# Weights rounded by casting transfers, their low parts made by adding transfers

## The chip, the cores and the metric

One core of a Trainium2 chip runs the kernel. The engines named in the profile are PE (the tensor engine, with its weight loads as PEld), DVE (vector), ACT (scalar), POOL (GpSimd) and SP (the engine that issues the transfers; SPq is its queue). The metric is the device time of one execution in microseconds (µs), lower is better.

## The reference

A two-layer encoder on x of 512 tokens by 1024 features, in float32. Each layer normalises its input, projects it with one matrix `w_in` (1024 by 4608) and splits the columns among three groups of heads: differential attention (A), retention with decays in both directions (B) and a pooling mixer (C). Each group is gated, and `w_out` (1536 by 1024) maps the three back onto the residual stream.

```
for l in range(2):
    h = rmsnorm(x, norm_w[l])
    aq, ak, av, ag, bq, bk, bv, bg, cu, cg = split(h @ w_in[l])
    o_a = diff_attention(aq, ak, av, rel_bias, lam, subln_w) * silu(ag)
    o_b = retention(bq, bk, bv, decay) * silu(bg)
    o_c = multiscale_pool(cu, pool_w, pool_scale) * silu(cg)
    x = x + concat(o_a, o_b, o_c) @ w_out[l]
out = rmsnorm(x, final_norm_w)
```

## The kernel before

**Two parts of every operand.** Matmuls run in the reduced type float32r. To keep float32's accuracy every operand is split in two: a high part, the value rounded to float32r, and a low part, the value minus the high part. A product is three matmuls (`mm3`): high by high, high by low, low by high. Weights are held as `wh` and `wl`.

**Granules.** The weights come in 96 granules of 128 partitions by 1024 elements, 0.5 MB each, in the order in which the units of a layer need them (the table `ORDERS`; a unit's name tells the columns of `w_in` or the blocks of `w_out`). A granule of a gate, a query or a key is 128 columns by all 1024 rows (eight pieces of 512 B in a partition); one of the values `bv`, `av` (four granules a unit) or of `w_out` is 256 rows by 512 columns (two pieces of 2 KB). The first unit of the program is `bv` of layer 0, granules 1 to 4.

**How one granule is made** (`emit_granule`): SP issues a transfer into a raw tile `wraw` (2 buffers), ACT casts it to `wh`, DVE subtracts `wh` from `wraw` into `wl` (`split`). `wh` and `wl` have 5 slots each (`WBUFS`). So the raw data of the next two granules is fetched while their slots are still in use. A unit takes its granules with `take`; 24 matmuls of 512 columns read a granule.

**What sets the order.** The program is first recorded; a list scheduler (`Recorder.schedule`) then fixes the order on every engine from planned costs (`cost`) and priorities, and gives each tile its slot. At run time each engine goes through its own list in order and waits where a semaphore tells it to: an instruction that waits holds up all that stand behind it on its engine. This holds for SP's and POOL's transfers too.

**Names around the change.** `hh`, `hl` are the parts of the normalised, transposed input; layer 0 runs on x transposed (`T<-in_xT_w`) with the weight of the norm alone, and each token's factor, the reciprocal root mean square, is applied to the products afterwards. That factor is made from `x` by ACT (squares), DVE and POOL (`st`, a power of -1/2, once for each of four token tiles), kept in `edge`, written to memory as `row` and read back on all partitions as `rb`. `pj` (3 banks), `lg` (2), `tp` (2) and `ov` (1) are the accumulation banks of the tensor engine. The heads' own norms take the same way (`st4`, `row`, `hn`). `wide` holds bias or decay tables, one buffer.

Of the kernel before, what the change touches and what calls it, by code (L numbers as in the profile page):

```python
# [9 lines left out]
F32 = mybir.dt.float32  # L10
# [19 lines left out]
# Order in which the units of a layer are recorded. An output unit is named by the pairs of 128-row blocks of w_out that it takes  # L30
# (A: P Q, B: R S, C: T U) and its half of the columns.
# [4 lines left out]
ORDERS = [o.split() for o in ORDERS]  # L36
PAIRS = {"P": ("A", 0), "Q": ("A", 2), "R": ("B", 0), "S": ("B", 2), "T": ("C", 0), "U": ("C", 2)}

# how far the units of a kind are moved ahead
# [4 lines left out]
# The kernel body is recorded first, on tiles that have no place yet. A list scheduler then fixes the order in which  # L44
# every engine issues its instructions and the slot each tile takes, and the program is emitted in that order.
# [17 lines left out]
class View:  # L63
    """Part of a recorded tile: partitions p0..p1, free offsets idx, and the steps that lead to it."""
# [32 lines left out]
    def window(self, row, first, pattern):  # L97
        """DRAM only: elements of a row from first on, by an access pattern of its own."""
        return View(self.base, self.p0, self.p1, self.idx, self.steps + (("window", row, first, pattern),))

    def spread(self, n):
        """Every element n times, along a new last axis."""
        return View(self.base, self.p0, self.p1, np.repeat(self.idx[..., None], n, -1), self.steps + (("spread", n),))
# [47 lines left out]
class Recorder:  # L151
# [9 lines left out]
    def add(self, name, engine, method, args, kw):  # L161
# [4 lines left out]
        ins = [v for v in list(args[1:]) + [x for k, x in kw.items() if k != "accum_out"] if isinstance(v, View)]  # L166
# [34 lines left out]
    def schedule(self):  # L201
# [39 lines left out]
        def ready(op):  # L241
            """A PSUM bank serves one engine at a time."""
# [55 lines left out]
WARM = 16  # matmuls on zeros at the start  # L298
QUEUE = 8  # transfers under way in a queue
FINE = 2  # weight granules of the first columns that come in two parts  # L300
# [3 lines left out]
def cost(engine, method, args, kw):  # L304
    """What an instruction weighs for the list scheduler: until its result stands, and on its engine."""
# [3 lines left out]
    if engine == "PE":  # L309
# [6 lines left out]
        return t, t  # L316
    if engine == "SP":
# [33 lines left out]
def record(ins: dict, out: bass.AP):  # L351
    nc = Recorder()
    x_d = ins["x"][0]
    w_in, w_out = ins["w_in"], ins["w_out"]
# [46 lines left out]
    def g_cols(l, c):  # L401
        return [w_in[l, :, c:c + P].rearrange("(k p) c -> p k c", p=P)]

    def g_tok(l, c):
        return [w_in[l, g * 256:(g + 1) * 256, c:c + 512].rearrange("(k p) c -> p k c", p=P) for g in range(4)]

    def g_out(l, e0, half):
        return w_out[l, e0:e0 + 256, HALF[half]].rearrange("(k p) c -> p k c", p=P)

    def unit_granules(l, u):  # L410
        if u in ("bv", "av"):
            return g_tok(l, BV if u == "bv" else AV)
        kind, i = u[:-1], int(u[-1])
        if kind in ("bg", "ag", "cu", "cg"):
            return g_cols(l, {"bg": BG, "ag": AG, "cu": CU, "cg": CG}[kind] + i * P)
        if kind == "bqk":
            return g_cols(l, BQ + i * P) + g_cols(l, BK + i * P)
        if kind == "qk":
            return g_cols(l, AQ + i * P) + g_cols(l, AK + i * P)
        if kind[0] == "o":  # L420
            return [g_out(l, "PQRSTU".index(c) * 256, i) for c in kind[1:]]
        return []

    granules = [g for l in range(DEPTH) for u in ORDERS[l] for g in unit_granules(l, u)]
# [3 lines left out]
    def emit_granule(parts=1):  # L428
        src = granules[len(wt)]
        shp = [P, src.shape[1], src.shape[2]]  # L430
# [28 lines left out]
    def square(t, half, junk, part=None):  # L459
        """Mean square of token tile t: the share of one half of its columns, or of a quarter in the second half."""  # L460
# [14 lines left out]
    def scaled(t, wb, dst, half):  # L475
        """One half of the columns of the rmsnorm of token tile t."""
        c = HALF[half]
        nc.vector.scalar_tensor_tensor(dst[:, c], xt[t][half], stats[t][:, 2:3], wb[:, c], op0=ALU.mult, op1=ALU.mult)

    def transpose4(src, step=None):  # L480
        """Four 128-column blocks of src, each transposed, in one bank."""
# [22 lines left out]
    def mm_stacked(ps, qk, m, cols):  # L504
        """Full product of slot m's query columns with its keys: both query parts lie stacked on partitions."""
# [16 lines left out]
    def stack_halves(dst, slots, src, scale, dup):  # L522
        """Split the 64 rows of each half of src. Without dup the low part goes to the other partition half of
        the same slot; with dup both parts take a slot each, present on both partition halves."""
# [13 lines left out]
    def headnorm(ov, scale, g):  # L538
        """ov * scale * rsqrt(mean over partitions of ov^2 + eps) * g"""
# [17 lines left out]
    def out_half(ms, half, after=None, before_end=None):  # L557
        """before_end: the last token tile comes in two quarters of the columns, and this follows the first."""
# [555 lines left out]
```

## Time and profile before

| | before |
|---|---|
| median of 3 runs, µs | 682.0 (681.04 to 682.2) |
| span of the profiled execution, µs | 679.9 |
| PE busy, µs | 659.5 |
| DVE busy, µs | 500.7 |
| ACT busy, µs | 353.9 |
| POOL busy, µs | 30.3 |
| DMA queue of SP, share of 16 engines | 36.3% |
| DMA, mean GB/s | 106 |

The profile is of one execution, whose span from the first to the last instruction stands above; the median is of whole runs. A busy engine is one that executes: waiting does not count. Matmuls overlap in their pipeline, so one that is listed with 0.39 µs starts 0.23 µs after the one before.

### The profile page before, as it was taken

Reading aid. Unit: us, or ns where it says so; the run is one execution under the profiler, and the core shown is the slowest. Engines: PE = TensorE matmul, PEld = TensorE weight load, DVE = VectorE, ACT = ScalarE, POOL = GpSimd, SP = SyncE. Lnnn points to the kernel's source line nnn. Section 1 sums busy time; section 2 is a strip of 40 time slices with the busy share of each in tenths; the row PEclk is TensorE's granted clock in tenths of the full one; section 3 lists DMA queues with packets and bytes.
Section 4 is the critical chain, followed back from the end, with each engine's and each line's share of the span. In section 5 each row is a group of like instructions: output and inputs, shape, how many; then the busy total and the mean of one; then the engine's idle time right before and its main releaser. Section 6 shows DMA issues by size and latency. Waiting matters only on the chain.

```text
span 679.9 us, 8912 instructions
## 1 busy us (share of the span) xinstructions
PE 659.5 (97%) x3171; PEld 541.1 (80%) x3171; DVE 500.7 (74%) x954; ACT 353.9 (52%) x701; POOL 30.3 (4%) x51
## 2 busy tenths in 40 slices
PE   9969999999999999999999999899999999999996
PEld 7757887878788888887888888688888887888785
DVE  5468987787787998976574779767568957887733
ACT  7525673434376866553443756344447765655321
POOL 0000000000000000001010000000000000000011
PEclk9979999999999999999999999999999999999999
DMA  9447444323326223243322423532342143224302
GB/s 325 147 127 186 139 115 117 110 94 78 90 50 181 77 91 105 69 115 91 115 63 78 139 64 88 131 118 71 95 122 65 50 150 97 71 92 90 99 31 94
DMA packets 85141, 71.86 MB, mean 106 GB/s; under 512 B 6004, under 2 KB 67604, under 8 KB 85096
## 3 DMA queue, kind: packets, MB, share of 16 engines
q1 hardware_dynamic: 85096, 71.29, 36.3%
q8 instruction: 25, 0.41, 0.2%
q14 instruction: 20, 0.16, 0.1%
HBM read 69.09 MB, written 2.18 MB: 105 GB/s over the span
## 4 chain that ended last, share of the span: by engine, by line
PE 78%; DMA 10%; DVE 6%; issue 2%; ACT 2%; SPq 1%; POOL 0%; POOLq 0%; DVEq 0%; ACTq 0%
PE pj L1051 64%; PE lg L1051 6%; PE ov L1051 4%; PE tp L1051 4%; DMA hn<-row 3%; DMA wide<-dd 2%; DVE qk L1051 1%; DMA row<-edge 1%; DVE soft L1051 1%; DMA wraw<-in_w_in 1%; DVE wl L1051 1%; DMA cols<-in_scales 1%; DMA T<-in_xT_w 1%; DMA x<-in_x 1%; ACT soft L1051 1%
## 5 line engine op out<-in xcount | busy, mean ns | idle before, releaser
L1051 PE MATMUL pj<-hh,wh 128*128 128x512 f32 x448 | 178.5, 400 | 7.9 <-ACT wh L1051 6.5
L1051 PE MATMUL pj<-hl,wh 128*128 128x512 f32 x448 | 177.5, 397 | 0.0
L1051 PE MATMUL pj<-hh,wl 128*128 128x512 f32 x448 | 176.9, 396 | 0.0
L1051 ACT CAST wh<-wraw 128x1024 fp32r<-128x1024 f32 (+1 forms) x97 | 100.8, 1039 | 106.9 <-PE pj L1051 75.8
L1051 DVE TENSOR_TENSOR wl<-wraw,wh 128x1024 fp32r<-128x1024 f32 (+1 forms) x97 | 117.3, 1210 | 29.7 <-ACT wh L1051 29.1
L1051 PEld LDWEIGHTS pj<-hh,wh 128*128 128x128 f32 x448 | 84.7, 189 | 27.1 <-ACT wh L1051 7.0
L1051 PEld LDWEIGHTS pj<-hh,wl 128*128 128x128 f32 x448 | 84.6, 189 | 18.6
L1051 PEld LDWEIGHTS pj<-hl,wh 128*128 128x128 f32 x448 | 84.7, 189 | 17.7
L1051 PE MATMUL pj<-wh,mAC 128*128 128x512 f32 (+1 forms) x264 | 87.5, 391 | 0.0
L1051 ACT ACTIVATE soft<-soft,sm 128x512 f32<-128x512 f32 x96 | 67.8, 718 | 33.9 <-DVE sm L1051 33.5
L1051 DVE TENSOR_TENSOR x<-x,pj 128x512 f32<-128x512 f32 (+1 forms) x65 | 43.6, 675 | 23.2 <-PE pj L1051 22.8
L1051 PEld LDWEIGHTS pj<-wh,mAC 128*128 128x128 f32 x264 | 49.0, 188 | 10.3
L1051 PE MATMUL lg<-qk 128*128 128x512 f32 (+1 forms) x192 | 51.4, 361 | 1.5 <-DVE soft L1051 1.5
L1051 PE MATMUL pj<-wl,mAC 128*128 128x512 f32 (+1 forms) x132 | 51.4, 389 | 0.0
L1051 POOL TENSOR_TENSOR st<-st,neghalf 128x4 f32<-128x4 f32 (+1 forms) x28 | 25.1, 896 | 477.3 <-DVE st L1051 379.2
L1051 DVE CUSTOM_DVE_ANT_0 soft<-lg,wide 128x512 f32<-128x512 f32 x64 | 43.3, 687 | 1.9 <-PE lg L1051 0.3
L1051 PE MATMUL pj<-wh,mB 128*128 128x512 f32 (+1 forms) x136 | 44.5, 383 | 0.0
L1051 PE MATMUL pj<-wh,hl 128*128 128x512 f32 x104 | 41.4, 398 | 0.0
L1051 PE MATMUL pj<-wh,hh 128*128 128x512 f32 x104 | 41.3, 398 | 0.0
L1051 PE MATMUL pj<-wl,hh 128*128 128x512 f32 x104 | 41.2, 396 | 0.0
L1051 PEld LDWEIGHTS lg<-qk 128*128 128x128 f32 x192 | 32.5, 188 | 9.6 <-DVE soft L1051 2.5
L1051 PE MATMUL ov<-T,vh 128*128 128x256 f32 x192 | 39.1, 284 | 0.4 <-DVE og L1051 0.3
(151 smaller groups left out, 949.7 us busy)
## 6 DMA issues: line engine op xcount, KB each, us to landing
wraw<-in_w_in SPq DMA_DIRECT2D x71, 512.0 KB, 4.6
wraw<-in_w_out SPq DMA_DIRECT2D x24, 512.0 KB, 4.1
hn<-row SPq DMA_DIRECT2D x16, 256.0 KB, 3.9
wide<-gd SPq DMA_DIRECT2D x8, 448.0 KB, 4.0
T<-in_xT_w SPq DMA_DIRECT2D x8, 258.0 KB, 4.1
x<-in_x SPq DMA_DIRECT2D x8, 256.0 KB, 5.0
wide<-dd SPq DMA_DIRECT2D x8, 256.0 KB, 4.8
out<-T SPq DMA_DIRECT2D x8, 256.0 KB, 2.1
```

The costliest lines, as they stand in the source:

```text
L1051: op.inst = getattr(getattr(tc.nc, name), method)(*[real(a) for a in op.args], **{k: real(v) for k, v in op.kw.items()})
```

## The change

From the fifth granule on, no raw tile is used. POOL issues a transfer from memory straight into `wh`; source and destination differ in type, so the transfer rounds. ACT then writes minus `wh` into `wl`. POOL issues a second transfer of the same source into `wl` that adds to what is there: the value minus the high part. DVE has no part in it. The first four granules are still made as before. The host lays all granules out as one array `wg`, in the order of use, so that a partition's 1024 elements lie in one row of 4 KB. The scheduler gets a planned cost for a POOL transfer, and an adding transfer is recorded as a reader of its destination.

```diff
+def weight_granules():
+    out = []
+    for l in range(DEPTH):
+        for u in ORDERS[l]:
...
+                out += [("w_in", l, (256 * g, BV if u == "bv" else AV), (2, 512)) for g in range(4)]
...
-        ins = [v for v in list(args[1:]) + [x for k, x in kw.items() if k != "accum_out"] if isinstance(v, View)]
+        kw_ins = [args[0]] if "accum_op" in kw else []
+        ins = [v for v in list(args[1:]) + [x for k, x in kw.items() if k != "accum_out"] + kw_ins if isinstance(v, View)]
...
+    if engine == "POOL" and method == "dma_start":
+        return 5500, 1500
...
-        src = granules[len(wt)]
-        shp = [P, src.shape[1], src.shape[2]]
+        at, (nk, nc_) = granules[len(wt)]
+        shp = [P, nk, nc_]
+        src = ins["wg"][at].rearrange("p (k c) -> p k c", k=nk)
+        if len(wt) >= 4:
+            hi = sb("wh", shp, WBUFS, F32R)
+            lo = sb("wl", shp, WBUFS, F32R)
+            nc.gpsimd.dma_start(hi, src)
+            nc.scalar.activation(lo, hi.bitcast(F32), AF.Copy, scale=-1.0)
+            nc.gpsimd.dma_start(lo, src, accum_op=ALU.add)
+            wt.append((hi, lo))
+            return
...
+    wg = np.empty((len(weight_granules()), P, 1024), np.float32)
+    for g, (name, l, (r, c), (nk, n)) in zip(wg, weight_granules()):
+        g[:] = np.asarray(inputs[name])[l, r:r + nk * P, c:c + n].reshape(nk, P, n).transpose(1, 0, 2).reshape(P, 1024)
+    a["wg"] = wg
```

**SP, the first 33 µs.** Numbers behind a name tell tiles apart. `row` and `rb` are the tokens' factor on its way out and back. Before:

```order
L1051 DMA x_0_242<-in_x 128x512
L1051 DMA x_0_253<-in_x 128x512
L1051 DMA wraw_262<-in_w_in 128x8x128
L1051 DMA wraw_276<-in_w_in 128x8x128
L1051 DMA soft_287<-in_decay 8x2
L1051 DMA row_319<-edge_112 128x4x1
L1051 DMA rb_339<-row_319 128x512
L1051 DMA wraw_348<-in_w_in 128x8x128
L1051 DMA wraw_397<-in_w_in 128x8x128
L1051 DMA wraw_408<-in_w_in 128x8x128
```

Now:

```order
L1059 DMA x_0_251<-in_x 128x512
L1059 DMA x_0_264<-in_x 128x512
L1059 DMA wraw_274<-in_pool_w 128x4x128
L1059 DMA wraw_288<-in_pool_w 128x4x128
L1059 DMA soft_299<-in_decay 8x2
L1059 DMA row_353<-edge_114 128x4x1
L1059 DMA rb_377<-row_353 128x512
L1059 DMA dd_476<-T_449 8x1024
L1059 DMA wide_493<-dd_476 128x2x256
```

The loads of weights that stood ahead of and behind `row` and `rb` are gone from SP; two early loads of `pool_w` stand in the first two places.

**POOL, the same place.** `st` with `neghalf` is the power for one token tile, `u` a margin that is zeroed; both lists begin behind the constants. Before:

```order
L1051 MEMSET u_67 128x8 x2
L1051 ISA
L1051 TENSOR_TENSOR st_172<-st_172,neghalf_65 128x1
L1051 TENSOR_TENSOR st_199<-st_199,neghalf_65 128x1
L1051 TENSOR_TENSOR st_279<-st_279,neghalf_65 128x1
L1051 TENSOR_TENSOR st_295<-st_295,neghalf_65 128x1
L1051 MEMSET u_511 128x8 x2
L1051 MEMSET u_576 128x8 x2
```

Now:

```order
L1059 DMA wh_67<-in_wg 128x1024
L1059 MEMSET u_93 128x8 x2
L1059 DMA wl_137<-in_wg 128x1024
L1059 DMA wh_187<-in_wg 128x1024
L1059 ISA
L1059 TENSOR_TENSOR st_177<-st_177,neghalf_65 128x1
L1059 DMA wh_247<-in_wg 128x1024
L1059 TENSOR_TENSOR st_206<-st_206,neghalf_65 128x1
L1059 DMA wl_254<-in_wg 128x1024
L1059 DMA wh_303<-in_wg 128x1024
L1059 TENSOR_TENSOR st_291<-st_291,neghalf_65 128x1
L1059 DMA wl_308<-in_wg 128x1024
```

The four powers now stand among transfers: a second or third waits for a slot of `wh`, or for ACT's negation, before the next power can run.

**ACT, the first granules.** Before:

```order
L1051 ACTIVATE hh_104<-T_69 128x512
L1051 CAST wh_108<-wraw_79 128x512 x2
L1051 ACTIVATE hh_104<-T_91 128x512
L1051 ACTIVATE hh_104<-T_97 128x512
L1051 CAST wh_150<-wraw_100 128x1024
L1051 ACTIVATE hh_104<-T_102 128x512
```

Now:

```order
L1059 ACTIVATE hh_106<-T_69 128x512
L1059 CAST wh_110<-wraw_78 128x512 x2
L1059 ACTIVATE hh_106<-T_90 128x512
L1059 ACTIVATE wl_137<-wh_67 128x1024
L1059 ACTIVATE hh_106<-T_99 128x512
L1059 CAST wh_154<-wraw_102 128x1024
L1059 ACTIVATE hh_106<-T_104 128x512
```

The negation for the fifth granule stands ahead of the third tile of `hh` and of the second granule's cast.

**POOL, the seam between the layers,** where the four granules of layer 1's values (`bv`) let go of their slots within a few matmuls of each other (the first number after `wh` or `wl` is the slot). POOL's list held no transfers there; now:

```order
L1059 DMA wl_4_3169<-in_wg 128x1024
L1059 DMA wh_3_3250<-in_wg 128x1024
L1059 DMA wh_2_3259<-in_wg 128x1024
L1059 DMA wh_1_3268<-in_wg 128x1024
L1059 DMA wh_0_3279<-in_wg 128x1024
L1059 DMA wl_3_3287<-in_wg 128x1024
L1059 DMA wl_2_3298<-in_wg 128x1024
L1059 DMA wl_1_3309<-in_wg 128x1024
L1059 DMA wh_4_3322<-in_wg 128x1024
L1059 DMA wl_0_3319<-in_wg 128x1024
```

Four rounding transfers stand in a row, then three adding ones.

**PE, the same seam.** Before:

```order
L1051 MATMUL pj_0_3287<-wl_0_3148,hh_0_3102 128x512
L1051 MATMUL pj_0_3287<-wh_0_3133,hl_0_3112 128x512
L1051 MATMUL pj_1_3326<-hh_0_3102,wh_4_3297 128x512
L1051 MATMUL pj_1_3326<-hl_0_3112,wh_4_3297 128x512
L1051 MATMUL pj_1_3326<-hh_0_3102,wl_4_3304 128x512
L1051 MATMUL pj_1_3326<-hh_0_3102,wh_4_3297 128x512
L1051 MATMUL pj_1_3326<-hl_0_3112,wh_4_3297 128x512
L1051 MATMUL pj_1_3326<-hh_0_3102,wl_4_3304 128x512
```

Now:

```order
L1059 MATMUL pj_1_3273<-hl_0_3066,wh_4_3116 128x512
L1059 MATMUL pj_1_3273<-hh_0_3058,wl_4_3169 128x512
L1059 MATMUL pj_1_3324<-hh_0_3058,wh_1_3268 128x512
L1059 MATMUL pj_1_3324<-hl_0_3066,wh_1_3268 128x512
L1059 MATMUL pj_2_3289<-hh_0_3058,wl_3_3287 128x512
L1059 MATMUL pj_2_3289<-hh_0_3058,wh_3_3250 128x512
L1059 MATMUL pj_2_3289<-hl_0_3066,wh_3_3250 128x512
L1059 MATMUL pj_2_3289<-hh_0_3058,wl_3_3287 128x512
```

The first projection behind the values (`pj_1_3326`) took the high and the low part of its granule in consecutive matmuls; now a projection there does its first two matmuls with the high part (`pj_1_3324` here, `pj_2_3289` some twenty rows earlier), and goes on with the low part when other products have run.

## Rows read from the trace of the kernel before

**Rows 1.** The page: span, and part 1, busy µs and share by engine.
```profile
span 679.9 us, 8912 instructions
PE 659.5 (97%) x3171; PEld 541.1 (80%) x3171; DVE 500.7 (74%) x954; ACT 353.9 (52%) x701; POOL 30.3 (4%) x51
```

**Rows 2.** Waits of PE: waiting, waited for, µs in total, times, longest.
```profile
PE pj L1051 <- ACT wh L1051: 6.5, 1, 6.5
PE lg L1051 <- ACT T L1051: 1.6, 1, 1.6
...
PE pj L1051 <- DVE gate L1051: 1.3, 1, 1.3
```

**Rows 3.** Timeline (start, duration, what, idle before): the tail.
```profile
668.26 0.69 DVE L1051 TENSOR_TENSOR x<-x,pj 128x512 f32<-128x512 f32 x1 [1.78 <-PE pj L1051]
...
669.08 1.31 POOL L1051 TENSOR_TENSOR soft<-x,T 128x512 f32<-128x512 f32 x1 [4.05 <-issue]
...
673.64 0.28 PE L1051 MATMUL pj<-wh,mB 128*128 128x256 f32 x1
```

**Rows 4.** Windows: stretch: length, busy by engine (instructions), PEclk, DMA share, GB/s.
```profile
352.06:389.55 37.49, 37.49 (x163) 30.12 (x163) 19.79 (x26) 18.46 (x26) 0.00 (x0) 1.00 0.34 98
```

**Rows 5.** Timeline around 33 µs: SPq, PE, DVE and ACT, each on its own.
```profile
23.95 0.38 SPq L1051 DMA_DIRECT2D row<-edge  x1
32.24 0.34 SPq L1051 DMA_DIRECT2D rb<-row  x1
32.69 0.37 SPq L1051 DMA_DIRECT2D wraw<-in_w_in  x1
...
33.40 0.39 PE L1051 MATMUL pj<-hl,wh 128*128 128x512 f32 x1
40.33 0.80 PE L1051 MATMUL pj<-hh,wh 128*128 128x512 f32 x1 [6.54 <-ACT wh L1051]
...
43.48 0.39 PE L1051 MATMUL pj<-hl,wh 128*128 128x512 f32 x1
...
37.70 0.69 DVE L1051 TENSOR_TENSOR cos<-cos,rb 128x512 f32<-128x512 f32 x1 [7.48 <-DMA rb<-row]
...
39.05 1.21 DVE L1051 TENSOR_TENSOR wl<-wraw,wh 128x1024 fp32r<-128x1024 f32 x1
...
39.23 1.04 ACT L1051 CAST wh<-wraw 128x1024 fp32r<-128x1024 f32 x1 [9.84 <-DMA wraw<-in_w_in]
```

**Rows 6.** Windows around the wait.
```profile
4.80:30.70 25.90, 25.90 (x111) 21.08 (x111) 16.54 (x41) 18.41 (x34) 2.20 (x4) 1.00 0.79 274
...
40.30:42.40 2.10, 2.07 (x5) 1.69 (x6) 2.07 (x6) 0.17 (x1) 0.00 (x0) 0.50 0.44 127
```

**Rows 7.** Timeline of the second granule: ACT, then PE.
```profile
8.62 1.05 ACT L1051 CAST wh<-wraw 128x1024 fp32r<-128x1024 f32 x1 [0.56 <-DMA wraw<-in_w_in]
...
10.94 0.39 PE L1051 MATMUL lg<-wh,hh 128*128 128x512 f32 x1
```

**Rows 8.** Chain of waits near 438 µs, and PE's timeline there.
```profile
436.76 1.22 DVE wl L1051
...
438.58 1.14 DVE wl L1051
...
440.37 0.50 PE L1051 MATMUL pj<-hh,wh 128*128 128x512 f32 x1 [1.34 <-DVE gate L1051]
```

**Rows 9.** Groups by line: out<-in, count, busy µs, mean ns, idle before.
```profile
L1051 DVE TENSOR_TENSOR wl<-wraw,wh 128x1024 fp32r<-128x1024 f32 (+1 forms) x97 | 117.3, 1210 | 29.7 <-ACT wh L1051 29.1
L1051 ACT CAST wh<-wraw 128x1024 fp32r<-128x1024 f32 (+1 forms) x97 | 100.8, 1039 | 106.9 <-PE pj L1051 75.8 <-DMA wraw<-in_w_in 28.9 <-issue 1.8
...
L1051 DVE CAST qk<-qk 64x1024 fp32r<-64x1024 f32 x24 | 16.5, 689 | 0.7
```

**Rows 10.** The page, parts 3 and 6: a queue; issues, KB, µs to landing.
```profile
q1 hardware_dynamic: 85096, 71.29, 36.3%
...
wraw<-in_w_out SPq DMA_DIRECT2D x24, 512.0 KB, 4.1
```

More of the change, by code (lines that the diff above doesn't have):

```diff
@@ L36 @@
 ORDERS = [o.split() for o in ORDERS]
+def weight_granules():
+    out = []
+    for l in range(DEPTH):
+        for u in ORDERS[l]:
+            if u in ("bv", "av"):
+                out += [("w_in", l, (256 * g, BV if u == "bv" else AV), (2, 512)) for g in range(4)]
+                continue
+            kind, i = u[:-1], int(u[-1])
+            if kind in ("bg", "ag", "cu", "cg"):
+                out.append(("w_in", l, (0, {"bg": BG, "ag": AG, "cu": CU, "cg": CG}[kind] + i * P), (8, P)))
+            elif kind in ("bqk", "qk"):
+                out += [("w_in", l, (0, c + i * P), (8, P)) for c in ((BQ, BK) if kind == "bqk" else (AQ, AK))]
+            elif kind[0] == "o":
+                out += [("w_out", l, ("PQRSTU".index(c) * 256, 512 * i), (2, 512)) for c in kind[1:]]
+    return out
 PAIRS = {"P": ("A", 0), "Q": ("A", 2), "R": ("B", 0), "S": ("B", 2), "T": ("C", 0), "U": ("C", 2)}
@@ L353, in record @@
     x_d = ins["x"][0]
-    w_in, w_out = ins["w_in"], ins["w_out"]
     def sb(tag, shape, bufs=1, dt=F32, name=None):
@@ L398, in record @@
     ident = sb("ident", [P, P])
[L401 to L424, printed above, removed]
+    granules = [(i, shape) for i, (_, _, _, shape) in enumerate(weight_granules())]
     wt = []
@@ L1089, in _arrays @@
 def _arrays(inputs):
-    plain = ("x", "norm_w", "w_in", "diff_lambda", "pool_w", "w_out", "rel_bias", "final_norm_w")
+    plain = ("x", "norm_w", "diff_lambda", "pool_w", "rel_bias", "final_norm_w")
     a = {n: np.ascontiguousarray(inputs[n]) for n in plain}
```

## The prediction

> **What bounds the kernel now.** I read the page from the top: the span and the busy shares, then the tensor engine's waits, then the stretches in which those waits fall, then the DMA part. The tensor engine runs matmuls for 659.5 of 679.9 µs; the vector engine is busy for 74%, the scalar engine for 52%, POOL for 4% [rows 1]. So work taken off the vector engine is worth nothing in itself; only what the tensor engine waits for counts. It sits idle for 20.4 µs in all: 6 after its last matmul ends at 673.9, a little before its first, and 14.2 in ten waits (eight rows), of which one is 6.5 and the next 1.6 [rows 1 to 3]. In a dense stretch a 512-column matmul starts every 0.230 µs (163 in 37.49 µs) [rows 4]. The span is 2.1 µs below the median of 682.0; I work against the span and add 2.1 at the end.
>
> **The large wait, step by step.** The tensor engine stops at 33.79 and goes on at 40.33, released by the scalar engine's cast of a weight granule [rows 5]. The cast had waited 9.84 µs for its transfer, which the DMA queue issued only at 32.69, right behind the read-back of `rb` at 32.24; that one in turn waited for `row` to be written, issued at 23.95 [rows 5]. So the weights did not come late because the DMA was slow: they stood behind a wait on SP. On DVE the two low parts stood behind the same read-back (`cos<-cos,rb` at 37.70 after 7.48 idle, `wl` at 39.05) [rows 5]. After the wait the granted clock is 0.50 (the lower of the two levels, 1.2 of 2.4 GHz) from 40.30 to 42.40, after 6.5 µs without a matmul [rows 6]; seven matmuls take from 40.33 to 43.48 where seven at 0.230 would take 1.6, so that costs 1.5 more [rows 4, 5]. The place costs 6.7 + 1.5 = 8.2 µs.
>
> **What the change does there.** SP no longer carries weights after the fourth granule and DVE makes no low parts after it, so neither wait stands in front of them. The fifth to eighth granules are queued on POOL, where each waits for its own slot, and the fifth has a free one from the start. Gain: 8.2. What could come due instead is `rb` itself: the fourth POW on POOL, from which `row` is written, now stands behind transfers that wait for slots which the tensor engine lets go at about 11, 16 and 22 µs (24 matmuls each from 4.8), and behind the adding transfer of the seventh granule. I put `row` at 28 instead of 23.95 and `rb` at 42 instead of 37.7. The first three projections have a bank each (27.6 to 44.2 at 24 × 0.230), so the fourth needs `rb` applied to the first by 44; about 1 µs is left, more with a later start. I take 0 and keep 4 as the end.
>
> **What it costs at the start.** The first POOL transfer (0.52 MB) competes with the tiles that the first matmuls need. From 4.80 to 30.70 the DMA engines moved 274 GB/s at a busy share of 0.79 [rows 6], 347 at full share, so 0.52 MB is 1.5 µs. The scalar engine gets one more 1.05 µs instruction (the negation, priced as its cast) ahead of the second granule's cast, which ended at 9.67 and is read at 10.94 [rows 7]: 1.27 to spare. 1.5 + 1.05 - 1.27 = 1.3, and up to 1.2 more if the rounded weights land after 7.0, when the scalar engine would get to them. I take 2.0; the ends are 0 (hidden) and 4 (the adding transfer also delays the next tiles).
>
> **What moves per granule.** 92 of the 96 granules change. Removed: 92 DVE subtractions of 1.21 µs, 111 µs, beside the tensor engine but for one place: at 438 two of them (1.22 and 1.14) stand straight ahead of the `gate` for which the tensor engine waits 1.34 [rows 8]. I take that 1.3 as a gain, and nothing for the other eight short waits (at most 6.4 together), which end on things the change does not touch. The scalar engine's 92 casts of 1.04 become 92 negations of the same shape [rows 9]: no change. The SP queue loses 92 issues, POOL gains 184.
>
> **The chain to a low part.** Before, a granule is fetched ahead into `wraw`; once its slot is free, a cast (1.04) and a subtraction (1.21) give both parts [rows 9]. Now nothing is fetched ahead: slot free, rounding transfer, negation, adding transfer. No row shows a POOL transfer. The nearest is the `w_out` load from SP, also 0.5 MB in rows of 2 KB, 4.1 µs from issue to landing [rows 10]. Lower bound: 4.1 + 1.04 + 4.1 = 9.3. Upper bound: POOL's own issue takes as long as its longest instruction here, 1.31 against SP's 0.4 [rows 3, 5], +0.9 twice, and the adding transfer moves twice the bytes: the queue moved 71.29 MB in 36.3% of 679.9 µs [rows 10], 289 GB/s, so 1.8 more. That is 12.9. Queueing of issues at the places where four slots come free together may add to it, so I take **13**, near the upper bound.
>
> Against this stands the cover. Walking the new order with 0.230 µs per 512 columns (half of that for 256, 0.1 for 128), I took for each refill the tensor work between the last read of the old tenant and the first read of the new low part. The tightest are 11.4 and 11.6 (the seam of the layers, as the order shows), then 13.7; 14 are under 15, 30 under 18, out of 91. Adding the shortfalls, each pushing what follows: a chain of 12 costs 0.6, 13 costs 1.6, 14 costs 3.4, 15 costs 11, 16 costs 21, 18 costs 47. It is a cliff, and I stand 1 to 2 µs from its edge. I take 1.6.
>
> The queue before shows 1.8 µs of DMA time per 0.52 MB. By the Trainium skill, "DMA: Bandwidth & Descriptors" (Anatomy of one DMA — SWDGE (gpsimd) path), a transfer issued from GpSimd takes about 2.0 µs plus bytes over 436 GB/s, which is an estimate of 3.2 for a granule; no run here shows it yet. By that price the chain is some 8.7 with an adding transfer of double length, no low part is late, and the sum below would be 1.6 less.
>
> The vector engine runs 24 copies `qk<-qk` of 689 ns [rows 9]. A rule that speaks against the change is the Trainium skill's, "SBUF — State Buffer" (SBUF: two separate sides): while DVE runs such a copy in its two-port mode, GpSimd cannot write the descriptors of its own transfers. The chain would then be up to 0.7 longer where the two meet, and the sum some 1.3 more.
>
> **Capacity.** A dense stretch takes a granule every 24 × 0.230 = 5.5 µs. Two transfers of 1.8 to 3.6 µs of DMA time are 3.6 to 5.4, beside a share of 0.34 there that already holds one load [rows 4]: it fits, at the upper end barely. Over the span the DMA share goes from 36% to between 61% and 85%. POOL may spend 2.75 µs on an issue before it falls behind.
>
> **The end.** The last granule's low part is now read some 14 µs after its slot is free, so three token tiles end within about 3 µs where they came 24 × 0.230 = 5.5 apart, each waited for (`x<-x,pj` at 668.26 after 1.78 idle) [rows 3]. Three tiles' residual sums and norms pile up on DVE before the last one, which I price at one residual sum, 0.5 to 0.7: +0.5 (0 to 2).
>
> **Sum.** 679.9 - 8.2 + 2.0 - 1.3 + 1.6 + 0.5 = 674.5; + 2.1 = 676.6, so **677 µs**.
>
> **The rivals.**
>
> *The chain is longer than its cover* (slower). Place: every refill whose cover is under some 18 µs, first the seam and the output units. Price as above: break-even with the other terms (6.9 net gain without the 1.6) lies at a chain of 14.5; at 16 the time is 677 + 20 = 697, at 18 it is 722. For it: nothing is fetched ahead any more, no row has a casting or adding transfer, and POOL and the scalar engine issue in order, so a late rounding holds everything behind its negation. Against it: 12.9 is already the upper bound of the rows, and the queue is idle for two thirds of the time. Chance 0.30.
>
> *POOL cannot issue fast enough* (slower). If one issue takes 3.5 µs instead of at most 2.75, every dense stretch runs at POOL's pace: 7.0 for a granule instead of 5.5; if half of the 92 lie in such stretches, 46 × 1.5 = 69 µs, about 745. For it: nothing measured. Against it: the longest instruction POOL has here is 1.31. Chance 0.05.
>
> *The gain at 33 µs is given back at once* (same). The start takes its 4 and `rb` the other 4 of the 8.2: 677 + 2 + 4 = 683. For it: the DMA is 0.79 busy exactly there, and each tile's POW stands behind POOL's transfers. Chance 0.12.
>
> *Other waits go too* (faster still). SP's queue, freed of weights, also brings `wide` and `hn` sooner, and no low part is late: 677 - 1.6 - 6.4 = 669. Chance 0.08.
>
> **How the numbers follow.** The forecast has 0.45, with a range of its own from 672 (start free) to 681 (chain 14, start 4). 669 at the one end keeps the best case in; at the other the range must reach into the long chain, to 16, which is 698; left out are chains above that and POOL's limit, about 0.2 together. About 0.2% is what a measurement can tell from no change, 680.6 to 683.4. Faster: 0.43 of the forecast, 0.08, and 0.03 of the third rival, 0.54. Same: 0.02 of the forecast, 0.07 of the third rival, 0.01 of the first, 0.10. Slower: what is left of the three rivals that allow it, 0.29 + 0.05 + 0.02 = 0.36.
>
> **What would show it.** Right: no wait of the tensor engine near 33 µs, first projection work starting about 2 µs later than before, DVE near 390 µs busy, DMA share above 60%, and waits of `pj` on `wl` that add up to less than 4. The landing times of the two POOL transfers decide: together under 12 with the negation at 1.04, the forecast holds; 15 or more, and the first rival has won. A scalar engine that waits for `wh` while the tensor engine waits for something else behind it on the scalar queue would be the same rival in another coat. Wrong altogether: POOL busy near 100%, or a new wait for `rb` at 44.

## The result: slower, 750.5 µs

The changed kernel takes 750.5 µs (746.6 to 752.7), the kernel before 681.5 beside it on the same chip: a ratio of 1.0997 (95% interval 1.0963 to 1.103). The forecast was 677 with a range from 669 to 698; the time lies above it, and on the other side of no change.

The page of the changed kernel, its span, part 1 and part 3 (queue: packets, MB, share of the time of 16 DMA engines):

```profile
span 750.9 us, 8985 instructions
...
PE 681.7 (91%) x3171; PEld 551.1 (73%) x3171; DVE 405.2 (54%) x862; ACT 354.2 (47%) x701; POOL 163.6 (22%) x235
...
q0 software_dynamic: 26496, 96.48, 58.5%
q1 hardware_dynamic: 16680, 23.05, 12.1%
```

Against [rows 1] the span has grown by 71.0. The tensor engine accounts for all of it: it idles 750.9 - 681.7 = 69.2 instead of 20.4 (+48.8), and it is busy for 22.2 more with the same 3171 matmuls, at a mean granted clock of 0.960 instead of 0.994. DVE has lost 95.5 µs of work, and the kernel is slower all the same. The packets of the two queues take 70.6% of the 16 engines' span, not 36.3% [rows 10].

What the tensor engine waits for now (waiting, waited for, µs in total, times, longest); these are the five largest of 17 rows; all 17 add up to 62.5, against 14.2 before:

```profile
PE tp L1059 <- ACT hn L1059: 11.6, 3, 6.0
PE pj L1059 <- DVE soft L1059: 8.1, 1, 8.1
PE pj L1059 <- DVE u L1059: 5.7, 1, 5.7
PE pj L1059 <- DMA wl<-in_wg: 5.5, 6, 2.3
PE tp L1059 <- DMA soft<-dd: 4.9, 1, 4.9
```

The 6.5 on ACT's cast [rows 2] is gone, as intended. Of the new waits only 5.5 µs stand directly on low parts of weights, the product of the long chain that the change introduces. The large ones end on `hn` (the heads' norm), on `soft` and `u` (the first products, multiplied by `rb`) and on `soft<-dd` (a decay table): small transfers that SP issues and that the change doesn't touch. Not all of the rest is free of the chain, though. One wait of 2.5 µs ends on DVE's `soft`, and the chain of waits there (start, duration, what) leads back to a weight:

```profile
104.15 8.76 DMA wh<-in_wg
...
112.93 1.06 ACT wl L1059
...
114.02 0.58 ACT soft L1059
...
115.22 1.90 DVE soft L1059 x3
...
117.17 0.93 PE tp L1059 x4
```

ACT waits for `wh` before it can negate it, and the copy to `soft` stands behind that on ACT's list.

The DMA view of the same run says what became of them (KB each, median µs from issue to landing):

```profile
wh<-in_wg POOLq DMA_DIRECT2D x92, 512.0 KB, 5.1
wl<-in_wg POOLq DMA_DIRECT2D x92, 512.0 KB, 7.0
hn<-row SPq DMA_DIRECT2D x16, 256.0 KB, 5.0
...
T<-in_xT_w SPq DMA_DIRECT2D x8, 258.0 KB, 8.5
...
rb<-row SPq DMA_DIRECT2D x1, 256.0 KB, 8.8
...
row<-edge SPq DMA_DIRECT2D x1, 2.0 KB, 9.0
```

Before, the same view has 3.9 for `hn` and 5.4 for `rb`:

```profile
hn<-row SPq DMA_DIRECT2D x16, 256.0 KB, 3.9
...
rb<-row SPq DMA_DIRECT2D x1, 256.0 KB, 5.4
```

**One place from close by.** The norm of one head in the last units, in the changed kernel's timeline (start, duration, what, idle before), SPq, DVE and PE each on its own:

```profile
685.57 0.32 SPq L1059 DMA_DIRECT2D row<-st  x1
691.95 0.32 SPq L1059 DMA_DIRECT2D hn<-row  x1
...
697.99 0.69 DVE L1059 TENSOR_TENSOR og<-og,hn 128x512 f32<-128x512 f32 x1 [6.56 <-DMA hn<-row]
...
699.48 1.13 PE L1059 MATMUL tp<-ident,hn 128*128 128x128 f32 x4 [5.99 <-ACT hn L1059]
```

and the same head before:

```profile
622.33 0.34 SPq L1051 DMA_DIRECT2D row<-st  x1
...
624.10 0.45 SPq L1051 DMA_DIRECT2D hn<-row  x1
```

`row` is 2 KB. SP could issue its read-back 1.77 µs after the write before, and 6.38 after it now. The tensor engine has nothing left to do and waits 5.99.

**The first 75 µs.** Windows of the changed kernel (length, busy µs by engine PE, PEld, DVE, ACT, POOL with instructions, PEclk, DMA share, GB/s):

```profile
0.00:35.00 35.00, 30.92 (x124) 23.47 (x125) 12.82 (x29) 19.24 (x34) 7.25 (x16) 0.95 0.98 310
35.00:75.00 40.00, 21.34 (x78) 15.89 (x77) 17.76 (x56) 10.19 (x15) 6.89 (x13) 0.72 0.69 130
```

and of the kernel before:

```profile
0.00:35.00 35.00, 32.57 (x138) 25.51 (x138) 17.40 (x43) 21.11 (x38) 2.55 (x10) 1.00 0.67 229
35.00:75.00 40.00, 34.67 (x143) 27.86 (x144) 31.47 (x63) 19.61 (x27) 0.28 (x4) 0.91 0.57 161
```

By 75 µs the tensor engine has started 202 matmuls instead of 281, and the DMA is busy at 0.98 over the first 35 µs instead of 0.67. Counted at 0.230 each [rows 4] the lag is 18 µs, a quarter of the loss; an expectation below puts it at 24, from the stops and the lower clock. The mean granted clock from 35 to 75 is 0.72, so part of that stretch runs at 1.2 instead of 2.4 GHz. The timeline there, changed kernel, SPq, PE and DVE:

```profile
37.29 0.37 SPq L1059 DMA_DIRECT2D row<-edge  x1
46.30 0.34 SPq L1059 DMA_DIRECT2D rb<-row  x1
...
57.26 0.80 PE L1059 MATMUL pj<-hh,wh 128*128 128x512 f32 x1 [8.06 <-DVE soft L1059]
...
55.18 0.69 DVE L1059 TENSOR_TENSOR cos<-cos,rb 128x512 f32<-128x512 f32 x1 [12.78 <-DMA rb<-row]
```

In [rows 5] `row` was issued at 23.95 and DVE had `rb` at 37.70; here it is 37.29 and 55.18. The wait has moved from the weights to `rb`, and grown.

### The profile page after: what moved, and what is told of

It reads as the page before. It is cut to its first block, busy times and chain, and to the rows that moved or that the text cites. A ratio compares the mean times of both kernels' runs of the same rounds, so it can differ in the third digit from the quotient of the medians.

```text
span 750.9 us, 8985 instructions
## 1 busy us (share of the span) xinstructions
PE 681.7 (91%) x3171; PEld 551.1 (73%) x3171; DVE 405.2 (54%) x862; ACT 354.2 (47%) x701; POOL 163.6 (22%) x235
## 3 DMA queue, kind: packets, MB, share of 16 engines
q0 software_dynamic: 26496, 96.48, 58.5%
q1 hardware_dynamic: 16680, 23.05, 12.1%
## 4 chain that ended last, share of the span: by engine, by line
PE 41%; DMA 23%; issue 18%; DVE 7%; POOL 6%; ACT 4%; SPq 0%; POOLq 0%; ACTq 0%; DVEq 0%
PE pj L1059 34%; DMA wh<-in_wg 5%; DMA hn<-row 4%; PE lg L1059 3%; DMA row<-st 3%; POOL wl L1059 3%; DVE soft L1059 2%; PE tp L1059 2%; POOL wh L1059 2%; PE ov L1059 2%; DMA wide<-dd 2%; POOL st L1059 1%; DVE T L1059 1%; DMA T<-in_xT_w 1%; DMA row<-edge 1%
## 5 line engine op out<-in xcount | busy, mean ns | idle before, releaser
L1059 PE MATMUL pj<-hh,wh 128*128 128x512 f32 x448 | 181.4, 406 | 15.6 <-DVE soft L1059 8.1
L1059 PE MATMUL pj<-hh,wl 128*128 128x512 f32 x448 | 181.0, 407 | 2.4 <-DMA wl<-in_wg 2.4
L1059 PE MATMUL pj<-hl,wh 128*128 128x512 f32 x448 | 180.5, 404 | 0.0
L1059 POOL DMA_DIRECT2D wl<-in_wg x92 | 82.4, 896 | 231.5 <-ACT wl L1059 202.6
L1059 ACT ACTIVATE wl<-wh 128x1024 fp32r<-128x1024 f32 x92 | 96.6, 1057 | 57.4 <-DMA wh<-in_wg 50.8
L1059 PEld LDWEIGHTS pj<-hh,wh 128*128 128x128 f32 x448 | 86.7, 193 | 36.4 <-DVE soft L1059 8.8
L1059 POOL DMA_DIRECT2D wh<-in_wg x92 | 54.9, 597 | 249.1 <-PE pj L1059 241.7
L1059 PEld LDWEIGHTS pj<-hl,wh 128*128 128x128 f32 x448 | 86.6, 193 | 18.2
L1059 PE MATMUL pj<-wh,mAC 128*128 128x512 f32 (+1 forms) x264 | 90.1, 404 | 5.8 <-DVE mAC L1059 2.9
L1059 ACT ACTIVATE soft<-soft,sm 128x512 f32<-128x512 f32 x96 | 67.8, 719 | 37.0 <-DVE sm L1059 36.7
L1059 DVE TENSOR_TENSOR x<-x,pj 128x512 f32<-128x512 f32 (+1 forms) x65 | 43.8, 675 | 41.2 <-PE pj L1059 41.1
L1059 PEld LDWEIGHTS pj<-wh,mAC 128*128 128x128 f32 x264 | 50.9, 196 | 17.8 <-DVE mAC L1059 3.8
```

The source lines that it names most:

```text
L1059: op.inst = getattr(getattr(tc.nc, name), method)(*[real(a) for a in op.args], **{k: real(v) for k, v in op.kw.items()})
```

## The experiments

**Two theories.** A, contention: the transfers on POOL take time on the 16 DMA engines that the small transfers on SP need, and the tensor engine waits for those. B, the chain: slot free, rounding, negation, adding is too long, or POOL's and ACT's instructions wait in order behind it. Beside them stand two smaller candidates: the early transfers at the start, and the plan's costs for the new transfers (5500 and 1500 ns, against 5.1 and 7.0 µs landing, 0.6 and 0.9 on POOL).

| kernel | queue of POOL, % | both queues, % | ratio to before | interval |
|---|---|---|---|---|
| 4 KB rows only | 0 | 34.9 | 1.0003 | 0.9983 to 1.0022 |
| raw loads on POOL | 22.5 | 35.2 | 1.0138 | 1.0078 to 1.0198 |
| adding transfer cut to an eighth | 29.2 | 41.8 | 1.0278 | 1.024 to 1.0317 |
| second transfer not adding | 44.7 | 56.5 | 1.0603 | 1.0545 to 1.0661 |
| the change | 58.5 | 70.6 | 1.0997 | 1.0963 to 1.103 |
| kernel before + idle adding transfers | 36.2 | 66.2 | 1.1157 | 1.1121 to 1.1192 |
| change, from the eleventh granule | 55.2 | 67.8 | 1.086 | 1.08 to 1.092 |
| change, planned with measured costs | 57.3 | 69.2 | 1.1167 | 1.1133 to 1.1201 |

The share is the time that a queue's packets took, of 16 engines over the span. Each ratio is to the kernel before run beside it, whose median lay between 681.5 and 686.0.

The table does not sort by the share alone. With raw loads on POOL the kernel is 1.4% slower at an unchanged share, and with an eighth of the adding transfer 2.8% slower for 5.5 points more. The last of these has the changed kernel's order on the tensor engine, its POOL queue and its rounding transfers. So at most 2.8 of the ten per cent come with those; the rest comes with the second transfer.

**The host's rows alone.** The changed kernel with every granule made the old way, by SP, ACT and DVE:

```diff
-        if len(wt) >= 4:
+        if False:
```

> The kernel before, with the weights alone laid out in 4 KB rows; SP loads, scalar cast and vector subtraction as before. Theory A (what costs the changed kernel its time is the DMA time of POOL's transfers, which slow the small transfers that SP issues for the norms): the rows only shorten the loads, so 682 or a little less, 678 to 682. Theory B (what costs is the chain slot, rounding, negation, adding, with the engines that stand in line behind it): same, 678 to 682. If the layout itself were at fault: 700 or more.

686.05 beside 686.04, ratio 1.0003. The layout in 4 KB rows is neither gain nor loss.

**Raw loads on POOL.** As the last, but the raw loads from the fifth on are issued by POOL; cast and subtraction stay:

```diff
-            nc.sync.dma_start(raw[:, k, :], src[:, k, :])
+            (nc.sync if len(wt) < 4 else nc.gpsimd).dma_start(raw[:, k, :], src[:, k, :])
```

> As e1, but the raw loads are issued by POOL, plain (no rounding, no adding), ahead of their slots; scalar cast and vector subtraction as before. The wait of the tensor engine at 33 us should go, since SP's read-back of rb no longer holds up weights. A: DMA time per granule is 1.3 us on each engine instead of 4, so little contention: 672 to 680. B: data is fetched ahead, so no chain: 672 to 680. If weights on POOL's queue as such were at fault (powers behind transfers): 700 or more.

693.3, ratio 1.0138. Both theories had expected a gain here (672 to 680), and both missed. The wait at 33 µs is gone, and three waits of 1.8, 2.6 and 2.7 µs end at 46, 50 and 59, the first two behind `rb`, which comes back at 42.7. So this way of moving the weights to another queue already gives the gain back, with no more bytes than before. It is also another plan: with the loads on POOL the scheduler orders the tensor engine's matmuls anew, and which of the two costs the 1.4% is not shown.

**The second transfer without adding.** In the changed kernel:

```diff
-            nc.gpsimd.dma_start(lo, src, accum_op=ALU.add)
+            nc.gpsimd.dma_start(lo, src)
```

> The changed kernel with its second transfer not adding, a plain rounding copy of the same bytes into the low part (so the low part holds the high part and the product is not the reference's). The order of all engines is the same. Its 4 KB packets should take some 0.17 us instead of 0.33, its landing about 5 us instead of 7. A: the DMA share falls from 0.71 to about 0.5 and at least a third of the 70 us goes: 715 to 730. B: the chain is 2 us shorter, and the tensor engine waited for low parts directly for 5.5 us only; with what stands behind, 735 to 745.

727.65, ratio 1.0603. The tensor engine's 3171 matmuls stand in the order of the changed kernel, and the number of transfers is the same; their time on the DMA engines is less:

```profile
wh<-in_wg POOLq DMA_DIRECT2D x92, 512.0 KB, 4.5
wl<-in_wg POOLq DMA_DIRECT2D x92, 512.0 KB, 4.7
```

Adding alone costs four of the ten per cent. B could claim some of it too, since the two landings together are 2.9 µs shorter, so this does not decide alone.

**An eighth of the adding transfer.**

```diff
-            nc.gpsimd.dma_start(lo, src, accum_op=ALU.add)
+            nc.gpsimd.dma_start(lo[0:16], src[0:16], accum_op=ALU.add)
```

> The changed kernel with its adding transfer cut to 16 of 128 partitions (the low part of the other 112 stays minus the rounded weight, so the product is not the reference's). The order of all engines is the same. The second transfer's DMA time falls to an eighth. A: 700 to 715. B: the chain is shorter by some 3 us (transfers land in 3 to 4 instead of 7): 725 to 740.

705.4, ratio 1.0278. A's numbers held in both runs, B's in neither. Both runs leave out what makes the low part right; only their time is read.

**The DMA time without the change.** This run separates A from B. It is the kernel with 4 KB rows, weights by SP, cast and subtraction, in its own order on PE, DVE, ACT and SP (the plan counts the new instructions at next to nothing, so that it stays as it was). Added is, for each of 92 granules, an adding transfer on POOL into an array in memory that nobody reads; a copy of one element a partition lets it go when the high part stands:

```diff
+        if len(wt) >= 4:
+            nc.gpsimd.tensor_copy(pace, hi.bitcast(F32)[:, 0, 0:1])
...
+            nc.gpsimd.dma_start(spare[len(wt) % 4], ins["wg"][at], accum_op=ALU.add)
...
         wt.append((hi, lo))
```

> The kernel before with its weights in 4 KB rows, made by cast and subtraction, in the same order on PE, DVE, ACT and SP; added are 92 adding transfers on POOL, one a granule, issued when its high part stands, into a spare array in memory that nobody reads. The engines of the DMA then carry what they carry in the changed kernel, and no chain or order of the change is there. Contention (the transfers on POOL take engine time from the small transfers on SP): 715 to 735 us, waits of PE spread over the run as in the changed kernel, hn<-row landing in 4.5 us or more instead of 3.9. Chain and in-order waits of the change: 684 to 692, as the rows alone.

761.8, ratio 1.1157: more than the change itself, with no rounding transfer, no negation, no chain and no new order of the matmuls. B expected 684 to 692. A's mechanism is shown, though its number (715 to 735) was too low: here SP's own weight transfers suffer as well. POOL's longer list is not what delays the norms: each of its 28 powers starts within 0.3 µs of the DVE result that it needs (1.2 in the changed kernel). One thing is not as in the change. The idle transfers add into memory, not into the chip's own tiles, so the memory carries 221 GB/s instead of 159, and this run cannot tell the engines' time from the memory's. Its DMA view (first the queues: packets, MB, share):

```profile
q0 software_dynamic: 13248, 48.24, 36.2%
q1 hardware_dynamic: 29928, 71.29, 30.0%
...
HBM read 117.33 MB, written 50.42 MB: 221 GB/s over the span
...
wraw<-in_wg SPq DMA_DIRECT2D x95, 512.0 KB, 6.2
...
hn<-row SPq DMA_DIRECT2D x16, 256.0 KB, 4.8
```

and its waits on transfers:

```profile
ACT wh L1067 <- DMA wraw<-in_wg: 68.5, 27, 16.6
...
DVE og L1067 <- DMA hn<-row: 49.1, 13, 9.1
```

The same wait of DVE for the heads' norm is 17.4 µs before, 21.1 with an eighth of the adding transfer, 37.0 without adding, and 43.0 in the changed kernel. In these runs it grows with the share of both queues, but not in step: raw loads on POOL have 24.4 at 35.2%, and the last run of this section 53.2 at 69.9%. The median landing of `hn` does not sort the runs at all (4.9 with an eighth, 5.0 in the changed kernel).

**A late start.** The changed kernel with ten granules made the old way instead of four:

```diff
-        if len(wt) >= 4:
+        if len(wt) >= 10:
```

> The changed kernel, but the first ten granules, not four, come as before, so that POOL issues no transfer before the tokens' factor is back. If the early transfers on POOL make the loss of the first 75 us (24 us against before), most of it goes and the wait at 33 us of the kernel before comes back: 726 to 736 us, rb back by 42 us. If the loss there comes from elsewhere (the order of the plan, the 4 KB rows): 745 to 752.

742.05, ratio 1.086: between the two expectations. `rb` is there at 39.7, as expected, and the old wait is back:

```profile
PE pj L1059 <- ACT wh L1059: 7.9, 1, 7.9
PE tp L1059 <- DMA soft<-dd: 7.2, 1, 7.2
```

By 75 µs its tensor engine has been busy for 58.4 µs, against 52.3 in the changed kernel and 67.2 before. The early transfers make under half of the lag there; the ones on POOL begin at 49.6 µs, and the tensor engine then waits until 71.5 for the next small transfer (`soft<-dd`) instead.

**The plan's costs.**

```diff
-        return 5500, 1500
+        return (7000, 900) if "accum_op" in kw else (5100, 600)
```

> The changed kernel, planned with the durations that its trace shows: 5.1 us until a rounding transfer stands and 0.6 on POOL, 7.0 and 0.9 for an adding one, instead of 5.5 and 1.5 for both. If the plan's order (low parts read too early, powers behind transfers) makes a large part of the loss: 725 to 740 us. Contention: the engine time of the transfers is the same, 745 to 757.

762.7, ratio 1.1167: slower than the changed kernel, and above both expectations. So the plan's wrong costs are not what makes the loss; why the truer ones are worse I have not settled. The waits of 8.7 and 5.7 for `soft` and `u` stay, and one of 5.4 on a DVE tile before `lg` comes in. ACT waits 83.9 µs for `wh` there, against 50.8 in the changed kernel.

**The wait that the change was to remove.** The kernel with 4 KB rows, with `row` and `rb` issued by POOL (planned at 2500 and 600 ns), so that SP's weights do not stand behind them:

```diff
-                    nc.sync.dma_start(row.rearrange("(t p) -> p t", t=NT), self.rc)
-                    nc.sync.dma_start(self.rb, row.partition_broadcast(P))
+                    nc.gpsimd.dma_start(row.rearrange("(t p) -> p t", t=NT), self.rc)
+                    nc.gpsimd.dma_start(self.rb, row.partition_broadcast(P))
```

> The kernel before with its weights in 4 KB rows, and only row and rb of the tokens' factor issued by POOL instead of SP, so that SP's weights no longer stand behind them. If the wait at 33 us was the queue's order alone: that wait goes, rb is back by 40, 6 to 9 us less than before, ratio 0.987 to 0.992. If the next thing (rb itself, the fourth projection) is due at once: 0.997 to 1.003.

683.8, ratio 1.0004, and the reason is not the one the second expectation named: the wait for the weights itself is still there, 6.6 µs (8.8 with 4 KB rows alone, 6.5 in the kernel before). Its timeline, SPq and ACT:

```profile
27.07 0.34 SPq L1059 DMA_DIRECT2D wraw<-in_wg  x1
...
39.34 1.04 ACT L1059 CAST wh<-wraw 128x1024 fp32r<-128x1024 f32 x1 [9.92 <-DMA wraw<-in_wg]
```

The granule leaves SP at 27.07 now, not at 32.69 [rows 5] or, with 4 KB rows alone, at 36.82. ACT gets it at 39.34, against 39.23 and 41.56. Of a lead of 9.7 µs on the 4 KB rows alone, 2.2 are left. The DMA view of the stretch 27.2 to 38:

```profile
q1 hardware_dynamic: 96, 0.39, 91.9%
...
wraw<-in_wg SPq DMA_DIRECT2D x1, 512.0 KB, 12.2
```

The packets that start there hold 0.39 MB of weights and take 91.9% of the 16 engines over 10.8 µs, 1.65 µs a packet; over the whole run of this kernel such a granule lands in a median of 3.7 µs, not 12.2. What is under way beside it is `row`: 512 elements of 4 bytes, each to a place of its own in memory, 10.4 µs from issue to landing. In the kernel before, next to nothing is under way beside the write. The DMA view from 24.3 to 32, in 40 slices, with the one packet of instructions (8 KB):

```profile
DMA  1118590000000000000000000000000000000000
...
DMA packets 582, 0.03 MB, mean 5 GB/s; under 512 B 533, under 2 KB 581, under 8 KB 581
...
q14 instruction: 1, 0.01, 2.8%
```

The packets have all started by 25.5, and no further one starts before the read-back leaves at 32.24. So most of the 8 µs are not time of the engines' packets, and where they go no view here shows. The one packet of instructions takes 3.4 µs there (2.8% of 16 engines over 7.7 µs).

**The pieces of `row`.** Next I changed the pieces. In the kernel before (not the changed one), the factor is written as 128 pieces of 16 bytes, read back in that order and put in order by a DVE copy:

```diff
-                    nc.sync.dma_start(row.rearrange("(t p) -> p t", t=NT), self.rc)
-                    nc.sync.dma_start(self.rb, row.partition_broadcast(P))
+                    nc.sync.dma_start(row.rearrange("(p t) -> p t", t=NT), self.rc)
+                    by_p = soft()
+                    nc.sync.dma_start(by_p, row.partition_broadcast(P))
+                    nc.vector.tensor_copy(self.rb.rearrange("p (t q) -> p t q", t=NT), by_p.rearrange("p (q t) -> p t q", t=NT))
```

> The kernel before; only the tokens' factor is written to memory as 128 pieces of 16 bytes instead of 512 of 4 bytes, read back in that order, and put in order by one DVE copy of 128x512. If the write in 4-byte pieces is what takes 8 us and holds the engines of the DMA (taken off SP's queue it left the wait at 33 us as it was, with a weight transfer beside it that took 12.2 us): row lands in under 3 us instead of 8, the wait at 33 us falls from 6.5 to 0 to 2, ratio 0.987 to 0.992. If the time is the transfer's fixed cost or the next thing is due at once: 0.997 to 1.003.

674.7 beside 685.8, ratio 0.9845 (0.9818 to 0.9872): faster than both kernels. Timeline, SPq:

```profile
23.94 0.35 SPq L1053 DMA_DIRECT2D row<-edge  x1
26.46 0.33 SPq L1053 DMA_DIRECT2D soft<-row  x1
```

The read-back leaves 2.5 µs after the write, where it was 8.3 [rows 5], and the window from 35 to 75 has no idle tensor engine and no lower clock:

```profile
35.00:75.00 40.00, 40.00 (x181) 32.36 (x180) 35.23 (x65) 22.66 (x31) 0.28 (x4) 1.00 0.56 159
```

With the write at 2.5 µs the whole wait of [rows 5] is gone, and the packet of instructions beside it takes 0.9 µs, not 3.4. The gain is 11 µs between the medians taken side by side (9 to 12 by the interval) and 8.4 between the two profiled spans; I had put 8.2 on the place.

**The same edit in the changed kernel.** The diff is the same.

> The changed kernel with the same edit to the tokens' factor. If the way of that factor (row 9.0, rb 8.8 us) makes the waits of 48 to 73 us there: 738 to 745 us, rb back by 50 instead of 55. If the loss there comes from the other transfers alone: 747 to 753.

746.7, ratio 1.0912 (1.0846 to 1.0977), against 1.0997 (1.0963 to 1.103) for the change: the two intervals touch, so the gain lies somewhere between nothing and some 1.5%, and the time falls between the two expectations. The trace of the start is plain (the read-back leaves at 38.7 instead of 46.3, `rb` is there at 43.8, two waits of 4.4 µs are left where the changed kernel has 8.1, 5.7 and 4.9, and by 75 µs it has started 244 matmuls, not 202). Of the 42 matmuls, 9.7 µs, the end sees 4 to 6: part of the lead is lost again between 75 and 150, where the tensor engine is busy for 68.2 µs instead of 72.5.

## Why the prediction was wrong

**The step that failed: what a transfer costs the others.** In "Capacity" I compared sums: 3.6 to 5.4 µs of DMA time for a granule against 5.5 µs of tensor work, "it fits". The sum was right (58.5% of 750.9 over 92 granules is 4.8, and the share of 71% lies in my 61 to 85). What I drew from it was wrong. Traffic that fits still delays what arrives in between, and the kernel's path runs through small transfers, one after the other (`row` out, `hn` back, once a head). Past the start I put this at nothing; the only price I gave the traffic was the start cost of 2.0 (4 at the end of its range). The run with idle adding transfers shows that such traffic by itself makes a loss of the size of the whole; there the 512 KB weights on SP are late as well as the small transfers. How the 69 µs of the changed kernel divide between small transfers and late weights is not shown. The Trainium skill has the ground for it in "DMA: Bandwidth & Descriptors" (Issuing engines are not separate DMA queues): transfers that different engines issue run on the same 16 DMA engines and interleave. The trace agrees (`hn` lands in 5.0 µs instead of 3.9 in the median, and from `row` to `hn` it is 6.38 instead of 1.77 at the place above). The prediction used that page for the price of one transfer only.

**"Nothing for the other eight short waits ..., which end on things the change does not touch."** The same error from the other side. Some of them end on `hn`, on `soft` and on `T`, and `tp` on `hn` alone went from 1.2 to 11.6. Untouched instructions still share the DMA. The rival "Other waits go too" even had SP bring `hn` sooner; it came later.

**`rb`: "I take 0 and keep 4".** The mechanism was named (the fourth power stands late, `rb` is due at 44), the size was off. I put `row` at 28 and `rb` at 42; they were 37.29 and 55. The powers did not wait for POOL's transfers as I had it: the fourth waited for DVE.

```profile
36.14 0.94 POOL L1059 TENSOR_TENSOR st<-st,neghalf 128x1 f32<-128x1 f32 x1 [4.00 <-DVE st L1059]
...
29.31 6.25 DMA soft<-in_decay
```

The tiles of the input and of `x` came late (8.5 and 6.5 µs to land, 4.1 and 5.0 before). On top of that DVE's list stood until 35.58 behind `soft<-in_decay`, 64 bytes that took 6.25 µs (the second line, from the chain of waits); ACT had finished the last squares at 33.0. Then the write took 9.0 and the read 8.8. My rival "given back at once" had a price of 4 for `rb`; the lag at 75 µs is 18. A new wait for `rb` at 44 was also the sign that I had named for being wrong altogether; it came, at 49.

**The wait at 33 µs: right place, wrong cause.** "The weights did not come late because the DMA was slow: they stood behind a wait on SP." They did stand behind it, with idle DMA engines. But taking them out from behind it gained no time: then the granule itself took 12.2 µs beside the write. What made the place long was the write in pieces of 4 bytes. [rows 5] showed 8.3 µs for these 2 KB, and I read it as a wait and did not ask why it was so long. "DMA: Bandwidth & Descriptors" in the Trainium skill (Rules for kernel authors) has the rule: a last dimension that isn't contiguous becomes one descriptor for each element, so it should be laid out contiguous. The trace agrees (533 packets under 512 B in the view of 24.3 to 32), and with 16-byte pieces the write takes 2.5 µs instead of 8.3.

**The lower clock.** I priced it at one place (1.5). The mean granted clock is 0.960 over the changed kernel's run and 0.994 before. With two levels, 1.2 and 2.4 GHz, that is an estimated 60 µs at the lower one instead of 8, and it shows as 22.2 µs more busy time. It comes with the waits: 0.72 from 35 to 75 µs, where the longest ones stand, and 0.97 to 0.99 from 75 to 600.

**What held, and what nearly did.** The chain is 5.1 + 1.06 + 7.0 = 13.2 where I took 13. The waits for low parts are 5.5 µs, where I took 1.6 and set 4 as the limit; the two landings add up to 12.1, just past the 12 under which the forecast was to hold. The rival of the long chain, on which I spent most of my doubt, came in small, and once "in another coat": the 2.5 µs at 117, where ACT waits for `wh` and the tensor engine for what stands behind it on ACT. An adding transfer takes about twice a plain one. POOL's issue, 0.60 and 0.90 µs, lay under the bound of 1.31. DVE at 405 busy where I said near 390, and its relief worth nothing. The 1.3 at 438 did not come: `pj` waits 3.7 for `gate` now, in two places.

**What stays open.** The runs tell that the added DMA traffic is the cause, not which part of a transfer's way is contended (the engines' turns, or the memory behind them). Between the sum of both queues and the time there is no simple law: idle adding transfers at 66.2%, with SP's weights in the path too, cost more than the change at 70.6%. The 1.4% of the raw loads and up to 2.8% of the change are not traced to DMA time. And the plan with truer costs came out slower, without an explanation.

## What to carry to other kernels

Before moving work from a compute engine to the DMA, list the small transfers on whose return the bound engine waits, and price the new traffic by the delay of those, not by whether the bytes fit. An engine that is busy for 74% is no reason to spend DMA time as long as the bound engine hardly waits for it. And ask of a long transfer why it is long: 2 KB in 8 µs was worth 1.5% of this kernel, and it was to be had by the layout of one write.

## What the runs showed of the hardware

An adding transfer costs the DMA about double. With raw loads POOL's queue took 22.5% of 689.9 µs for 92 transfers, 1.7 µs of all 16 engines for one; with adding transfers alone, into memory, 36.2% of 760.7, 3.0 µs. A transfer that also rounds is not dearer than a plain one by any such factor: with both transfers of a granule rounding and none adding, 92 pairs took 44.7% of 722.8, 1.8 each. In the changed kernel a pair takes 4.8, which leaves 3.0 for the one that adds into the chip's own tiles.

A write of 2 KB in 4-byte pieces took 8.3 µs until its read-back could leave (11.2 with the weights in 4 KB rows), in 16-byte pieces 2.5. It also held up what was under way beside it: a packet of instructions took 3.4 to 3.7 µs in three runs, and 0.9 beside the 16-byte pieces. A granule beside such a write took 12.2 µs to land where 3.7 is usual, and its packets in that stretch took 1.65 µs each; that this too is due to the pieces is inferred, since no run here has the same granule beside 16-byte pieces.
